# Retention's output with three pairs of each block as sevens and three low parts by transfer; one more seven in feed-forward 2, blocks 5 and 7

## The chip, the cores and the metric

The kernel runs on one core of a Trainium2 chip. The metric is the device time of one execution in microseconds (us). Engines are named as the profile names them: PE is the matrix engine, PEld its weight loads, DVE the vector engine, ACT the scalar engine, POOL GpSimd, and SP the engine that issues most of the transfers (DMA).

## The reference

One decoder layer in float32 for 256 tokens of 2048 features: a first half feed-forward, two token mixers side by side, a second half feed-forward, and a gated per-layer embedding, each followed by a layer normalisation. What the change touches:

```python
ret_branch = (jax.nn.silu(rg) * ro) @ w_ret_out[i]
...
mixed = (jax.nn.sigmoid(gate_r) * ret_branch + jax.nn.sigmoid(gate_a) * att_branch) @ w_mix_out[i]
h = layer_norm(alpha * h + mixed, ln_g[i, 1], ln_b[i, 1])
h = layer_norm(alpha * h + 0.5 * swiglu(h, w_ffn2_gu[i], w_ffn2_down[i]), ln_g[i, 2], ln_b[i, 2])
```

`w_ret_out` and `w_mix_out` are 2048 x 2048; `w_ffn2_gu` is 2048 x 11264.

## The kernel before, in words

**Two halves of a number.** Every float32 product is made of three matmuls. A value is split into a high part, which PE takes as it is, and a low part, the value less its high part. `Sum.add` (L407 to L420) issues, for a product of two such pairs, low times high, high times high and high times low into one bank (L418, L419, L420). All matmuls in question have a moving operand of 128x512.

**Chunks and units.** Weights come in chunks of 128x1024 float32 (512 KB), loaded by SP (L113). The weights of a matrix product of 2048 rows are walked in eight pairs p = 0 to 7 of 256 rows, and each pair has two chunks (n = 0, 1) for a block of 1024 columns. A unit is what is taken in one go:

- `Single` (P, L153): one chunk. ACT casts the high part (L124), DVE subtracts for the low part (L128). 12 matmuls; a pair is two such units, 24 matmuls.
- `Transferred` (T, L170): the second chunk of a pair. ACT writes the negative of the raw chunk, rounded as PE takes it (L133), and POOL issues a transfer that adds the raw chunk to it in place (L134): what is left is the low part, made without DVE. ACT casts the high part afterwards. It begins three units ahead of its use (`lead = 3`). The first chunk of a T pair is a `Single`.
- `Seven` (S, L181): both chunks of a pair as one, with seven block products in place of eight (Strassen's scheme, in the form that shares sums). 21 matmuls. DVE makes four sums of 128x512 (L208, L209, L210, L213), four low parts (L128, L215, L216, L217); ACT makes four casts (L124, L199, L211, L214). It needs forms of the other operand, made once for two pairs by `forms_of` (L504 adds, L492 to L495, and a split at L99 and L100).
- `Prepared` (D, L228): a seven whose sums were made and written to DRAM long before. It loads 2.75 MB (a chunk, half of the other, and four sums, L113, L236, L240) and costs DVE two low parts (L128, L252).

A `block` (L448) takes a list of units in order, a letter and a pair each, and accumulates their products into banks; at the end of its last seven `seven_common` (L523: one ACT copy L526, four DVE operations L527 to L530) folds the shared sums, and then DVE adds what the plain units left in the banks. `units_of` (L511) gives the letters S the pairs of a given list, the letters D those that were prepared ahead, and P and T the rest in order.

**Order.** The engines run the program in its order, each its own part. All loads stand in a plan that runs over the whole kernel, so that SP issues loads of the next blocks as slots come free; a load waits for its slot's last reader. After every unit taken, `run_side` (L354) takes one job off a list, `side`, that holds small work beside the matmuls; `along(n, job)` (L942) puts a job n units ahead. So side jobs go by units finished, across the bounds of blocks.

**The mixers' end.** `mixers` (L1193) ends with: the gate blocks; the attention output in four steps (banks ma0 to ma3, operands att_t), after whose second the retention forms `made[0]` are made (tiles mrf); the retention output in two blocks mr0 and mr1, `mixer_block` (L1207), each over eight pairs of `w_ret2`, in the order RET_UNITS; and the mix product, `w_mix`, in four blocks (banks mo0 to mo3). `mixer_block` ends with four additions on DVE (L1214: the shared result tiles eve, evw plus the banks mr1a, mr1b); then each half is multiplied with its gate sig (L1575) and the attention's part is added (L1576). The results sig0 to sig3 are what the mix product takes; they have to be turned first, into mixt0 to mixt7. sig0 and sig1, ready after mr0, go by words through transposing transfers (`by_words`, `by_turns`, L1543 to L1551): a copy on ACT, a transfer by SP four units later, a join on ACT, and then the job `mixed` that splits the turned tile (high part L99 on ACT, low part L100 on DVE): mixt0 and mixt1 from sig0, mixt2 and mixt3 from sig1. Counted from mr1's first unit, that job runs after the 13th unit for sig0 and after the 14th for sig1. sig2 and sig3 are turned on PE (L1541, banks mxt) during the mix, as side jobs behind these. The first unit of mo0 takes mixt0, the second mixt1, the third mixt2, and so on.

**Feed-forward 2.** `ffn` (L971) walks eleven blocks j of 512 gate and 512 up columns; `gu_units` (L899) gives the order of units of each. Blocks 1 to 5 and 7 are in AHEAD and have prepared sevens, in pairs 4 and 5 (blocks 2 and 4 in pair 4 alone); SEVEN are the pairs 0 to 3 that can be sevens in place. Blocks 6 and 8 to 10 have the order PTSSPSST. The banks of block 5 are f2g5, f2u5 and f25s.

Of the kernel before, what the change touches and what calls it, by code (L numbers as in the profile page):

```python
# [41 lines left out]
SEVEN = (0, 1, 2, 3)  # L42

AHEAD = {1: (4, 5), 2: (4,), 3: (4, 5), 4: (4,), 5: (4, 5), 7: (4, 5)}
# [12 lines left out]
def layer(ctx: ExitStack, tc: tile.TileContext, io):  # L57
# [13 lines left out]
    def banks(name):  # L71
        return [bank(name + str(j)) for j in range(2)]

    def slot(shape, dt, name):
        return slots.tile(shape, dt, tag="slot", name=name)
# [364 lines left out]
    def block_units(units, keys):  # L440

        for kind, p in units:
            if kind in "PT":
                plan.extend((Transferred if kind == "T" and n else Single)(keys(n, p)) for n in range(2))
            else:
                plan.append((Seven if kind == "S" else Prepared)(keys(0, p), keys(1, p)))
# [38 lines left out]
    def seven_forms(full, hi, lo):  # L485


        a11, a21 = (full[:, 0::2, t * P : (t + 1) * P] for t in range(2))
        a12, a22 = (full[:, 1::2, t * P : (t + 1) * P] for t in range(2))
        raw = slot([P, 8, P], F32, "sums")  # L490
        f5, f6, f7, f3 = (raw[:, 2 * j : 2 * j + 2, :] for j in range(4))
        dve.tensor_tensor(f5, a21, a22, ALU.subtract)  # L492
        dve.tensor_tensor(f7, a11, a21, ALU.subtract)
        dve.tensor_tensor(f6, f5, a11, ALU.subtract)
        dve.tensor_tensor(f3, a12, f6, ALU.add)  # L495
        split(hi, lo, raw)
        return lambda e: [(hi[:, 2 * j + e, :], lo[:, 2 * j + e, :]) for j in range(4)]

    def whole(parts, name):

        full = slot([P, 4, S], F32, name)
        n = 4 // len(parts)
        for j, v in enumerate(parts):
            dve.tensor_tensor(full[:, n * j : n * j + n], v[:, :, :S], v[:, :, S:], ALU.add)  # L504
        return full

    def forms_of(parts, name):
        hi, lo = (slot([P, 8, P], F32R, name + w) for w in "hl")
        return seven_forms(whole(parts, name + "w"), hi, lo)

    def units_of(order, sevens, ahead=()):  # L511

        sevens, ahead = list(sevens), list(ahead)
        plain = [p for p in range(KD // 2) if p not in sevens + ahead]
        of = {"S": sevens, "D": ahead, "P": plain, "T": plain}
        return [(kind, of[kind].pop(0)) for kind in order]
# [25 lines left out]
    def paired_out(key, n_k, lhs, ps, before=None):  # L542

        sums = [Sum(ps[t], n_k) for t in range(2)]
        for c in range(n_k // 2):
            if before is not None and c % 2 == 0:
                before(c // 2)
            u = take(key + (c,))
            tokens_chunk(u.chunk, 2 * c, lhs, sums, (0, 1))
            done(u)  # L550
            run_side()
# [347 lines left out]
    def gu_units(name, j):  # L899
        if j == 0:  # L900
            return [("P", p) for p in range(KD // 2)]
        if name == "f2" and j in AHEAD:
            return units_of(*(("PPSDSDSP", SEVEN[:3]) if j % 2 else ("PPSSDSSP", SEVEN)), AHEAD[j])
        return units_of("PTSSPSST", SEVEN)

# [28 lines left out]
    def plan_ffn(name):  # L934
        for j in range(KF // 4):
            block_units(gu_units(name, j), gu_keys(name, j))
        first, second, held = down_units(HELD_PAIRS[name == "f2"])
        block_units(first, down_keys(name, 0))
        block_units(second, down_keys(name, 1))
        plan.extend(Single(down_keys(name, 1)(n, p)) for n in range(2) for p in held)  # L940
# [215 lines left out]
    SH_A = [i + 8 if i < 8 else i - 8 if i < 16 else i for i in range(32)]  # L1156

    GATE_UNITS = units_of("PPSSPSSP", (0, 1, 2, 3))
    RET_UNITS = units_of("PPPSPSPP", (0, 1))
    VALUE_UNITS = units_of("PSPSSPSP", (0, 1, 2, 3))  # L1160
    gate_keys = lambda b: lambda n, p: ("w_in_f2", 29 + 4 * b + 2 * n, p)
    value_keys = lambda n, p: ("w_rv", 1 + n, p)
# [2 lines left out]
    def plan_mixers():  # L1165
# [16 lines left out]
        for b in range(2):  # L1182
            block_units(RET_UNITS, ret_keys(b))
        for blk in range(4):
# [8 lines left out]
    def mixers(ht, norm, residual, keepers, away):  # L1193
# [10 lines left out]
        made = {}  # L1204
# [59 lines left out]
        ret_t = [None] * HR  # L1264
# [107 lines left out]
        for h in range(0, HR, 2):  # L1372
# [3 lines left out]
            g = slot([P, 2, 512], F32, f"rgs{h}")  # L1376
# [154 lines left out]
        def of_pairs(v, k):  # L1531
            a = v[k // 2][:, k % 2, :]
            return a[:, :S], a[:, S:]
# [26 lines left out]
        for j in range(4):  # L1560
            v = sig[4 + j]
            act.activation(v, v, AF.Sigmoid)
            pa = banks(f"ma{j}")
            paired_out(("w_att2", 2 * j), KD // 2, lambda k: of_pairs(att_t, k), pa)
            for t in range(2):
                dve.tensor_tensor(v[:, t], v[:, t], pa[t], ALU.mult)
            if j == 1:
                made[0] = forms_of(ret_t[:2], "mrf")
        for b in range(2):
            for v in sig[2 * b : 2 * b + 2]:  # L1570
                act.activation(v, v, AF.Sigmoid)
            pr = mixer_block(f"mr{b}", RET_UNITS, ret_keys(b), lambda k: of_pairs(ret_t, k))
            for n in range(2):
                j = 2 * b + n
# [345 lines left out]
```

## Time and profile before

| | us |
|---|---|
| median of three executions | 2248.71 (2248.48 to 2250.64) |
| the profiled execution, whole | 2247.44 |
| its span, first to last instruction | 2245.6 |
| mr0, on PE | 1275.60 to 1317.76 |
| mr1, on PE | 1317.76 to 1359.92 |
| feed-forward 2 block 5, on PE | 1664.6 to 1705.9 |
| feed-forward 2 block 7, on PE | 1747.8 to 1787.9 |
| mean granted clock of PE | 0.999 |

Times inside the kernel count from the span's start. Rows of the timeline show start, duration, engine, line, operation, tiles and, in brackets, how long the engine had been idle and what released it. Rows of the waits show the waiting engine and what it writes, whom it waited for, and the sum, the number and the longest. Matmuls overlap, so a row's duration is longer than the distance between two starts.

### The profile page before, as it was taken

The page shows a single profiled execution, that of the slowest core. Times are in us where ns is not written, and L with a number is a line of the kernel's source. Part 1 is how long each engine was busy: PE and PEld are TensorE (multiplying, and loading weights), DVE is VectorE, ACT ScalarE, POOL GpSimd, SP SyncE. Part 2 cuts the span into 40 slices and gives each one's busy share as a digit, 9 for nine tenths or more (in the row PEclk, how much of TensorE's full clock was granted, in tenths as well). Part 3 has the DMA queues.
Part 4 walks back from the last instruction along what each step waited for, and adds up shares of the span by engine and source line. Part 5 has one row for each costly group of instructions (what it writes and reads, how often), then busy time and mean ns, then how long its engine had stood idle before and what let it go on. Part 6 is the DMA issues. An engine that isn't in the chain of part 4 may idle for free.

```text
span 2245.6 us, 28810 instructions
## 1 busy us (share of the span) xinstructions
PE 2231.5 (99%) x10195; PEld 1846.5 (82%) x10195; DVE 1995.4 (89%) x2636; ACT 1390.7 (62%) x1642; POOL 26.7 (1%) x37
## 2 busy tenths in 40 slices
PE   9999999999999999999999999999999999999998
PEld 8888888888888788888788888788887887888887
DVE  7999999999988999898779778789998999889877
ACT  6776767766554644566866456456666677655543
POOL 0000000000000000000000000000000000000000
PEclk9999999999999999999999999999999999999999
DMA  9787887765677778986657579788979978656772
GB/s 316 225 262 241 230 257 234 225 243 182 224 286 262 242 258 306 308 254 206 191 164 246 170 218 322 260 289 258 319 241 273 311 228 248 220 195 219 289 266 73
DMA packets 285946, 548.22 MB, mean 244 GB/s; under 512 B 87644, under 2 KB 92124, under 8 KB 285800
## 3 DMA queue, kind: packets, MB, share of 16 engines
q1 hardware_dynamic: 279784, 529.11, 70.7%
q0 software_dynamic: 4032, 14.68, 3.5%
q10 hardware_dynamic: 1984, 2.58, 0.3%
q8 instruction: 80, 1.31, 0.2%
q14 instruction: 66, 0.54, 0.1%
HBM read 484.43 MB, written 29.36 MB: 229 GB/s over the span
## 4 chain that ended last, share of the span: by engine, by line
PE 90%; DVE 6%; DMA 2%; issue 1%; ACT 1%; ACTq 0%; DVEq 0%; SPq 0%; POOL 0%; POOLq 0%
PE f1g L420 3%; PE f1g L418 3%; PE f1g L419 3%; PE rqk L369 3%; PE f1u L420 2%; PE f1u L418 2%; PE f1u L419 2%; PE f2g L418 2%; PE f2g L420 2%; PE f2g L419 2%; PE f2u L418 2%; PE f2u L420 2%; PE f2u L419 2%; PE aqk L369 2%; PE f2d L420 2%; PE f1d L419 2%
## 5 line engine op out<-in xcount | busy, mean ns | idle before, releaser
L124 ACT CAST hf_gu<-rf_gu 128x1024 fp32r<-128x1024 f32 x264 | 271.4, 1047 | 45.5 <-DMA rf_gu<-in_f_gu 38.6
L128 DVE TENSOR_TENSOR lf_gu<-rf_gu,hf_gu 128x1024 fp32r<-128x1024 f32 x236 | 281.5, 1217 | 14.6 <-ACT hf_gu L124 13.4
L124 ACT CAST hf_down<-rf_down 128x1024 fp32r<-128x1024 f32 x150 | 153.0, 1050 | 61.1 <-DMA rf_down<-in_f_down 50.2
L128 DVE TENSOR_TENSOR lf_down<-rf_down,hf_down 128x1024 fp32r<-128x1024 f32 x150 | 178.0, 1218 | 13.1 <-ACT hf_down L124 5.9
L128 DVE TENSOR_TENSOR lw_in_f<-rw_in_f,hw_in_f 128x1024 fp32r<-128x1024 f32 x140 | 167.0, 1217 | 2.8 <-ACT hw_in_f L124 2.7
L124 ACT CAST hw_in_f<-rw_in_f 128x1024 fp32r<-128x1024 f32 x140 | 141.9, 1050 | 24.9 <-DMA rw_in_f<-in_w_in_f 14.9
L214 ACT CAST hvf_gu<-vf_gu 128x1024 fp32r<-128x1024 f32 x76 | 80.1, 1054 | 84.8 <-DVE vf_gu L213 75.1
L211 ACT CAST huf_gu<-uf_gu 128x1024 fp32r<-128x1024 f32 x76 | 80.0, 1053 | 53.8 <-DVE uf_gu L209 50.5
L216 DVE TENSOR_TENSOR luf_gu<-uf_gu,huf_gu 128x1024 fp32r<-128x1024 f32 x76 | 92.4, 1216 | 1.6 <-ACT huf_gu L211 1.6
L217 DVE TENSOR_TENSOR lvf_gu<-vf_gu,hvf_gu 128x1024 fp32r<-128x1024 f32 x76 | 92.4, 1216 | 0.0
L418 PE MATMUL f1g<-hf_gu,xt 128*128 128x512 f32 x232 | 90.7, 391 | 0.0
L419 PE MATMUL f1g<-hf_gu,xt 128*128 128x512 f32 x232 | 90.5, 390 | 0.0
L420 PE MATMUL f1g<-lf_gu,xt 128*128 128x512 f32 x232 | 90.5, 390 | 0.0
L418 PE MATMUL f2g<-hf_gu,ht 128*128 128x512 f32 x214 | 83.5, 390 | 0.0
L420 PE MATMUL f2g<-lf_gu,ht 128*128 128x512 f32 x214 | 83.3, 389 | 0.0
L419 PE MATMUL f2g<-hf_gu,ht 128*128 128x512 f32 x214 | 83.3, 389 | 0.0
L418 PE MATMUL f1u<-hf_gu,xt 128*128 128x512 f32 x192 | 74.7, 389 | 0.0
L419 PE MATMUL f1u<-hf_gu,xt 128*128 128x512 f32 x192 | 74.7, 389 | 0.0
L420 PE MATMUL f1u<-lf_gu,xt 128*128 128x512 f32 x192 | 74.7, 389 | 0.0
L418 PE MATMUL f2u<-hf_gu,ht 128*128 128x512 f32 x168 | 65.7, 391 | 0.0
L420 PE MATMUL f2u<-lf_gu,ht 128*128 128x512 f32 x168 | 65.4, 389 | 0.0
L419 PE MATMUL f2u<-hf_gu,ht 128*128 128x512 f32 x168 | 65.4, 389 | 0.0
(1622 smaller groups left out, 6729.0 us busy)
## 6 DMA issues: line engine op xcount, KB each, us to landing
rf_gu<-in_f_gu SPq DMA_DIRECT2D x360, 512.0 KB
rf_down<-in_f_down SPq DMA_DIRECT2D x176, 512.0 KB
rw_in_f<-in_w_in_f SPq DMA_DIRECT2D x148, 512.0 KB
rw_rv<-in_w_rv SPq DMA_DIRECT2D x32, 512.0 KB
rw_ret<-in_w_ret SPq DMA_DIRECT2D x32, 512.0 KB
rw_mix<-in_w_mix SPq DMA_DIRECT2D x32, 512.0 KB
rw_pg<-in_w_pg SPq DMA_DIRECT2D x32, 512.0 KB
lf_gu<-rf_gu POOLq DMA_DIRECT2D x28, 512.0 KB, 7.8
```

The lines of the kernel that those rows point to most:

```text
L124: act.copy(self.hi, self.raw)
L128: dve.tensor_tensor(self.lo, self.raw, self.hi, ALU.subtract)
L211: act.copy(uh, u)
L214: act.copy(vh, v)
L216: dve.tensor_tensor(ul, u, uh, ALU.subtract)
L217: dve.tensor_tensor(vl, v, vh, ALU.subtract)
L369: pe.matmul(ps[f], hi[:, kk, f * P : (f + 1) * P], rhs(k), start=k == 0, stop=k == n_k - 1,)
L418: pe.matmul(o, al, bh, start=first, stop=False)
L419: pe.matmul(o, ah, bh, start=False, stop=False)
L420: pe.matmul(o, ah, bl, start=False, stop=self.left == 0)
```

## The change

The order of units of the retention output goes from PPPSPSPP with pairs 0 and 1 as sevens to PTSTSTSP with pairs 0, 1 and 2 as sevens: per block one plain pair becomes a seven, and of the five pairs that stay plain three have the low part of their second chunk made by transfer. The third seven's pair needs a second set of forms, `made[1]`, from ret_t[2:4]; it is made after the last step of the attention output. Feed-forward 2 blocks 5 and 7 go from PPSDSDSP with three sevens in place to PSDSSDSP with four. Blocks 1 and 3 keep their order: of the blocks in AHEAD, `j > 4` selects 5 and 7.

```diff
         if name == "f2" and j in AHEAD:
+            if j > 4:
+                return units_of("PSDSSDSP", SEVEN, AHEAD[j])
             return units_of(*(("PPSDSDSP", SEVEN[:3]) if j % 2 else ("PPSSDSSP", SEVEN)), AHEAD[j])
...
-    RET_UNITS = units_of("PPPSPSPP", (0, 1))
+    RET_UNITS = units_of("PTSTSTSP", (0, 1, 2))
...
-            if j == 1:
-                made[0] = forms_of(ret_t[:2], "mrf")
+            if j in (1, 3):
+                g = j // 2
+                made[g] = forms_of(ret_t[2 * g : 2 * g + 2], f"mrf{g}")
```

A retention block has 13 units in place of 14, a changed feed-forward block 10 in place of 11. On PE the program has 9,970 rows in place of 9,982.

On DVE, at the end of mr1, the rows before. lw_mix_0_3 and lw_mix_0_4 are low parts of the mix's weights, eve and evw the result tiles of mr1, sig2 and sig3 the gates:

```order
L128 TENSOR_TENSOR lw_mix_0_3_12265<-rw_mix_0_3_12178,hw_mix_0_3_12237 128x1024
L100 TENSOR_TENSOR mixt2_12269<-mxraw1_12128,mixt2_12269 128x2x256
L100 TENSOR_TENSOR mixt3_12272<-mxraw1_12128,mixt3_12272 128x2x256
L1214 TENSOR_TENSOR eve_12180<-eve_12180,mr1a0_11924 128x512
L1214 TENSOR_TENSOR eve_12180<-eve_12180,mr1b0_11926 128x512
L1214 TENSOR_TENSOR evw_12181<-evw_12181,mr1a1_11925 128x512
L1214 TENSOR_TENSOR evw_12181<-evw_12181,mr1b1_11927 128x512
L1575 TENSOR_TENSOR sig2_10380<-sig2_10380,eve_12180 128x1024
L1576 TENSOR_TENSOR sig2_10380<-sig2_10380,eve_11222 128x1024
L1575 TENSOR_TENSOR sig3_10574<-sig3_10574,evw_12181 128x1024
L1576 TENSOR_TENSOR sig3_10574<-sig3_10574,evw_11223 128x1024
L128 TENSOR_TENSOR lw_mix_0_4_12302<-rw_mix_0_4_12203,hw_mix_0_4_12263 128x1024
```

The same place on DVE in the changed program (its lines have numbers 2 or 3 higher there):

```order
L1216 TENSOR_TENSOR eve_12254<-eve_12254,mr1a0_11952 128x512
L1216 TENSOR_TENSOR eve_12254<-eve_12254,mr1b0_11954 128x512
L1216 TENSOR_TENSOR evw_12255<-evw_12255,mr1a1_11953 128x512
L1216 TENSOR_TENSOR evw_12255<-evw_12255,mr1b1_11955 128x512
L1578 TENSOR_TENSOR sig2_10380<-sig2_10380,eve_12254 128x1024
L1579 TENSOR_TENSOR sig2_10380<-sig2_10380,eve_11222 128x1024
L1578 TENSOR_TENSOR sig3_10574<-sig3_10574,evw_12255 128x1024
L1579 TENSOR_TENSOR sig3_10574<-sig3_10574,evw_11223 128x1024
L128 TENSOR_TENSOR lw_mix_0_4_12334<-rw_mix_0_4_12250,hw_mix_0_4_12293 128x1024
L100 TENSOR_TENSOR mixt2_12338<-mxraw1_12184,mixt2_12338 128x2x256
L100 TENSOR_TENSOR mixt3_12341<-mxraw1_12184,mixt3_12341 128x2x256
```

The split into mixt2 and mixt3 has moved from in front of mr1's last additions to behind them, the gate operations and a low part of the mix's weights.

On SP, in feed-forward 2 block 5, the rows before, of pair 1 (a seven), pair 5 (prepared), pair 2 (the last seven) and pair 7 (plain):

```order
L113 DMA rf2_gu_5_0_1_14965<-in_f2_gu 128x2x512
L113 DMA rf2_gu_5_1_1_14967<-in_f2_gu 128x2x512
L113 DMA rf2_gu_5_0_5_15057<-in_f2_gu 128x2x512
L236 DMA rf2_gu_5_0_5b_15059<-in_f2_gu 128x2x256
L240 DMA huf2_gu_5_0_5_15061<-hudf2_gu_5_0_5_8927 128x1024
L240 DMA luf2_gu_5_0_5_15063<-ludf2_gu_5_0_5_8928 128x1024
L240 DMA hvf2_gu_5_0_5_15065<-hvdf2_gu_5_0_5_8929 128x1024
L240 DMA lvf2_gu_5_0_5_15067<-lvdf2_gu_5_0_5_8930 128x1024
L113 DMA rf2_gu_5_0_2_15097<-in_f2_gu 128x2x512
L113 DMA rf2_gu_5_1_2_15099<-in_f2_gu 128x2x512
L113 DMA rf2_gu_5_0_7_15122<-in_f2_gu 128x2x512
```

The same place on SP in the changed program, where pair 2 and pair 3 are sevens and pair 3 is the last:

```order
L113 DMA rf2_gu_5_0_1_14954<-in_f2_gu 128x2x512
L113 DMA rf2_gu_5_1_1_14956<-in_f2_gu 128x2x512
L113 DMA rf2_gu_5_0_2_14970<-in_f2_gu 128x2x512
L113 DMA rf2_gu_5_1_2_14972<-in_f2_gu 128x2x512
L113 DMA rf2_gu_5_0_5_15102<-in_f2_gu 128x2x512
L236 DMA rf2_gu_5_0_5b_15104<-in_f2_gu 128x2x256
L240 DMA huf2_gu_5_0_5_15106<-hudf2_gu_5_0_5_8927 128x1024
L240 DMA luf2_gu_5_0_5_15108<-ludf2_gu_5_0_5_8928 128x1024
L240 DMA hvf2_gu_5_0_5_15110<-hvdf2_gu_5_0_5_8929 128x1024
L240 DMA lvf2_gu_5_0_5_15112<-lvdf2_gu_5_0_5_8930 128x1024
L113 DMA rf2_gu_5_0_3_15145<-in_f2_gu 128x2x512
L113 DMA rf2_gu_5_1_3_15147<-in_f2_gu 128x2x512
```

Two chunks of pair 2 have come in front of the six loads of the prepared pair 5, and the last seven behind these is pair 3.

## Prediction

> **What bounds the kernel now.** The profile's page was read first: TensorE (PE) is at work nearly all the time.
>
> ```profile
> span 2245.6 us, 28810 instructions
> PE 2231.5 (99%) x10195; PEld 1846.5 (82%) x10195; DVE 1995.4 (89%) x2636; ACT 1390.7 (62%) x1642; POOL 26.7 (1%) x37
> ```
>
> The profiled execution took 2247.44 us, 1.8 more than its span and 1.3 less than the median of 2248.71. Sums below are made against the execution and carried over to the median. Second, PE's timeline gives the price of a matmul, here at the seam between the two retention-output blocks mr0 and mr1:
>
> ```profile
> 1317.53 0.39 PE L420 MATMUL mr0b<-lw_ret,rett 128*128 128x512 f32 x1
> 1317.76 0.39 PE L418 MATMUL mr1a<-hw_ret,rett 128*128 128x512 f32 x1
> ```
>
> Each row shows 0.39 us, but starts are 0.227 apart; that is what one costs. A plain weight unit (12 matmuls) is 2.72 us, a seven (21) 4.76 us where its plain pair (24) is 5.44. Third, the waits of PE: the longest and two of the ends of sevens that speak below; those left out are of 1.4 us and less each, so hardly any idle time can be won back.
>
> ```profile
> PE lnps L670 <- DVE mixy L658: 2.0, 2, 1.5
> ...
> PE f25s L420 <- DVE luf_gu L216: 0.4, 1, 0.4
> PE f26s L420 <- DVE luf_gu L216: 0.3, 1, 0.3
> ```
>
> So what counts is the number of matmuls, and whether DVE, which makes the low parts, stays ahead. Fourth, the windows of the two stages that are touched (mr0, mr1; then feed-forward 2 blocks 5, 6, 7; columns PE, PEld, DVE, ACT, POOL busy, then PE's granted clock, full in all, DMA's share, GB/s):
>
> ```profile
> 1275.60:1317.80 42.20, 42.20 (x188) 34.95 (x187) 31.99 (x37) 21.97 (x23) 0.00 (x0) 1.00 0.62 200
> 1317.80:1359.90 42.10, 42.10 (x187) 34.87 (x186) 37.53 (x43) 27.81 (x31) 0.00 (x0) 1.00 0.79 252
> ...
> 1664.60:1705.90 41.30, 40.71 (x178) 33.08 (x177) 33.70 (x42) 25.86 (x29) 0.86 (x1) 1.00 0.88 289
> 1705.90:1747.80 41.90, 41.41 (x182) 33.65 (x181) 40.02 (x49) 29.53 (x32) 0.86 (x1) 1.00 0.87 258
> 1747.80:1787.90 40.10, 40.10 (x178) 33.21 (x177) 34.80 (x43) 25.54 (x29) 0.89 (x1) 1.00 0.89 296
> ```
>
> DVE has some 10 us to spare in mr0, 4.6 in mr1, 7.6 in block 5, 5.3 in block 7, and 1.9 in block 6.
>
> **The matmuls removed.** Four new sevens, each for a plain pair, remove 3 matmuls each: 12 x 0.227 = 2.72 us, 1.36 in retention, 0.68 in each of blocks 5 and 7. That is 0.12%, less than the 0.2% (4.5 us) which a measurement of this kernel can tell from no change.
>
> **Retention's units.** A seven's DVE work, and what it costs more than a plain pair, stands in block 5's last seven: from the first row's start to the last row's is 6.42 us; the two low parts of a pair are 2.27 (2.35 less the overlap).
>
> ```profile
> 1690.82 0.69 DVE L208 TENSOR_TENSOR uf_gu<-rf_gu 128x512 f32<-128x512 f32 x1 [6.29 <-DMA rf_gu<-in_f_gu]
> ...
> 1697.24 2.35 DVE L128 TENSOR_TENSOR lf_gu<-rf_gu,hf_gu 128x1024 fp32r<-128x1024 f32 x2
> ```
>
> Per block, DVE had 12 low parts (13.6 us) and 2 sevens (12.9): 26.5. It now has 7 low parts (7.9), since three are transferred, and 3 sevens (19.3): 27.2. The surplus of 0.7 disappears in the spare time above. A second set of forms is added at the end of the attention output, which the rows of the first set price:
>
> ```profile
> 1254.64 1.29 DVE L504 TENSOR_TENSOR mrfw<-rett 128x512 f32<-128x512 f32 x2
> ...
> 1259.84 2.35 DVE L128 TENSOR_TENSOR lw_att<-rw_att,hw_att 128x1024 fp32r<-128x1024 f32 x2
> ```
>
> That is 5.2 us of DVE from the first row to the last, a wait on ACT in it, from about 1276.4 on, in front of mr0's first seven. This seven now begins on PE at 1275.6 + 4 x 2.72 = 1286.5 and needs its first sum's low part about 2 us later; DVE can have it at 1276.4 + 5.2 + 5.3 = 1286.9. It holds by about 1.6 us: nothing on the path. If that cover is gone, it costs what it is late.
>
> The six transferred low parts leave DVE and are a multiplication on ACT and an accumulating transfer, whose rows in feed-forward are:
>
> ```profile
> L133 ACT ACTIVATE lf_gu<-rf_gu x2: 1054/1056/1057, 1699.3 to 1732.2; 128x1024 fp32r<-128x1024 f32 x2
> ...
> lf_gu<-rf_gu POOLq DMA_DIRECT2D x28, 512.0 KB, 7.8
> ```
>
> They start three units ahead. In retention those are, for the last two, a plain unit, a seven and a plain unit: 2.72 + 4.76 + 2.72 = 10.2 us, for 1.05 + 7.8 = 8.85. With 1.3 us in hand, and ACT's queue in front, a late one costs 0 to 2 us. DMA has room there (shares 0.62 and 0.79 above). I take 0.3 for all six, near nothing, since none of that row's 28 stands among PE's waits.
>
> **The hidden cost: one unit less in mr1.** The side jobs go by units finished. mr1 now has 13 instead of 14 units, and the job that splits the second gated tile into mixt2 and mixt3 runs on the 14th, after the first unit of the mix. Thus on DVE it now stands behind the four additions that end mr1 (L1214), the four gate operations (L1575, L1576) and one low part. The prices are at the end of mr0, where PE went on with mr1 at 1317.76:
>
> ```profile
> 1317.96 0.69 DVE L1214 TENSOR_TENSOR evw<-evw,mr0b 128x512 f32<-128x512 f32 x1
> ...
> 1323.36 2.35 DVE L128 TENSOR_TENSOR lw_ret<-rw_ret,hw_ret 128x1024 fp32r<-128x1024 f32 x2
> ...
> 1358.35 1.29 DVE L100 TENSOR_TENSOR mixt<-mxraw,mixt 128x512 fp32r<-128x512 f32 x2 [2.00 <-ACT mixt L99]
> ```
>
> With E the end of mr1 on PE: the gate operations end at E + 5.60 (1323.36 - 1317.76), the low part takes 1.14 (half of the pair's 2.27), mixt2's low part 0.68: E + 7.42. PE has two units of the mix without mixt2, 2 x 2.72 = 5.44 us, and must then wait: 1.98 us. In before the split ran at 1358.35, in front of L1214 and 7 us ahead of its use. The order on DVE is fixed, and its last addition cannot come before PE's last matmul of mr1, so I see no way round this; after it mixt3 (0.6 more) is in time.
>
> A stop of PE may also cost clock. These rows are PE's at its wait in the value product, and at the normalisation behind the mix:
>
> ```profile
> 774.63 0.40 PE L419 MATMUL rvss<-huw_rv,rvf1h 128*128 128x512 f32 x1
> 776.35 0.50 PE L420 MATMUL rvss<-luw_rv,rvf1h 128*128 128x512 f32 x1 [1.32 <-DVE luw_rv L216]
> ...
> 778.29 0.62 PE L420 MATMUL rvss<-luw_rv,rvf1h 128*128 128x512 f32 x1
> 778.71 0.63 PE L418 MATMUL rvsa<-hw_rv,ht 128*128 128x512 f32 x1
> ...
> 781.70 0.40 PE L419 MATMUL rvsb<-hvw_rv,ht 128*128 128x512 f32 x1
> ...
> 1448.67 0.39 PE L420 MATMUL mo<-lw_mix,mixt 128*128 128x512 f32 x1
> 1450.60 0.44 PE L670 MATMUL lnps<-ident,mixy 128*128 128x128 f32 x2 [1.55 <-DVE mixy L658]
> ...
> 1452.03 0.39 PE L419 MATMUL pp<-hw_pp,pt 128*128 128x512 f32 x1
> ```
>
> After the first, of 1.72 us between starts, matmuls stood 0.43 apart for 3.4 us: 8 matmuls at 0.2 more, 1.6 to 1.7 us lost. After the second, of 1.93, there was nothing. So the range is 0 to 1.7; by one case in two I leave it out of the likeliest sum and make it a rival. [...]
>
> **Blocks 5 and 7.** DVE's work rises by 6.42 - 2.27 = 4.15 us in each. Its waits there are the cover:
>
> ```profile
> DVE uf_gu L208 <- DMA rf_gu<-in_f_gu: 6.3, 1, 6.3
> DVE lf_gu L128 <- ACT hf_gu L124: 1.2, 1, 1.2
> ...
> DVE uf_gu L208 <- DMA rf_gu<-in_f_gu: 4.0, 1, 4.0
> DVE lf_gu L128 <- ACT hf_gu L124: 1.1, 1, 1.1
> ```
>
> (the first two of block 5, the last two of block 7.) 7.5 and 5.1 us cover 4.15, if the last seven's chunks land when they did. They stand on SP behind the six loads of the second prepared seven:
>
> ```profile
> 1675.68 0.37 SPq L113 DMA_DIRECT2D rf_gu<-in_f_gu  x1
> ...
> 1679.76 2.03 SPq L113 DMA_DIRECT2D rf_gu<-in_f_gu  x2
> ```
>
> They landed 11 us later (1690.82, above), and from then DVE was behind: PE's waits in f25s and f26s follow. The new order moves the prepared loads behind two more chunks of the new seven; they wait for a slot that PE frees when the first seven ends (1674.4 by my count instead of 1675.7), and the last chunks for the end of the first prepared one (1679.6 instead of 1679.8). So the landing moves by -1.5 to 0 us in block 5; in block 7, whose gap is smaller, by -0.3 to +1.9. As the DVE chain behind each landing sets PE's time, the 0.68 us of matmuls saved ahead of it is not kept: PE waits in f25s instead. Together I take 0, between -1.8 and +1.9.
>
> **The sum** on the profiled execution: -1.36 (retention's matmuls) + 1.98 (mixt2) + 0.3 (transfers) + 0 (blocks 5, 7) = +0.9: 2248.3; on the median 2249.6.
>
> **The rivals.**
> - *All matmuls kept, no new wait*: mixt2 is in time by something I overlook, and blocks 5 and 7 keep their savings: -2.72, 2246.0. For it: PE-bound page; against it: DVE's order. Chance 0.10. If the waits of f25s and f26s go as well (about 2.2 us with what follows them), 2243.8: 0.03.
> - *The wait costs clock too*: +0.9 + 1.7 = 2251.3. For it the value product, against it the normalisation. Chance 0.25.
> - *Blocks 5 and 7 land late* (the other side): if the last seven's chunks land over 3.6 us later in total, DVE's chain, with 1.9 us spare in block 6 and no more behind block 7, hands all of it to PE, and the kernel is slower than 2253.2; with 2.6 later in each, +0.9 + 5.2: 2254.8. Against it: SP issues them no later by my count. Chance 0.07.
> - *Transfers late*: ACT's queue puts each of the six back by 2.3 us, 1 more than is in hand: six times 1 us instead of the 0.3, so 2249.6 + 5.7 = 2255.3. Against it: the 28 of before, of which none holds PE. Chance 0.04.
>
> **The numbers.** Forecast 0.51, +0.9: 2249.6. From the first rival to a little above the clock rival, with the unknown of blocks 5 and 7: 2246.0 to 2252.9 leaves out some 0.17. Faster by over 0.2% (below 2244.2) 0.03; slower (above 2253.2) 0.10; within 0.87.
>
> **What would show it.** PE: 9,970 matmul rows of code for 9,982; a wait of about 2 us at the mix's third unit (mo, L418) put down to DVE mixt L100; mr0 and mr1 0.68 us shorter each, without a wait on rf or lw_ret transfers; half-spaced matmuls behind the wait or none. DVE: idle before L208 down to some 2 us in block 5 and about 1 in block 7. It is wrong if no such wait stands there, or if the waits at the last sevens, f25s to f210s, sum to over 2 us more or less than before.

## The result, and the profile after

The changed kernel takes 2252.41 us (median of 20 executions, 2251.15 to 2255.21), the kernel before on the same chip 2248.33 (20 executions). The ratio is 1.0017, with a 95% interval of 1.0010 to 1.0023: slower by 3.8 us (2.2 to 5.2). That is within the range, within 0.2%, and on the side that was forecast, but four times the 0.9 of the sum. Microseconds beside a ratio are, from here on, the ratio's distance from 1 times 2248.5.

The profiled execution of the changed kernel took 2252.14 us (before: 2247.44). The page's head, to be held against the first rows of the prediction:

```profile
span 2250.4 us, 28851 instructions
PE 2232.2 (99%) x10183; PEld 1843.8 (82%) x10183; DVE 2008.4 (89%) x2661; ACT 1402.5 (62%) x1657; POOL 31.9 (1%) x43
```

Twelve matmuls fewer, as planned, and yet PE is busy for 0.7 us longer: either matmuls have become slower or the rows of idle time have not caught all. Where the time went is read from the starts of stages on PE, each the first matmul of its bank in PE's timeline:

| stage begins on PE | before | after | later by |
|---|---|---|---|
| mr0 | 1275.60 | 1275.29 | -0.31 |
| mr1 | 1317.76 | 1316.77 | -0.99 |
| mr1 ends (0.227 after the start of its last matmul) | 1359.92 | 1358.25 | -1.67 |
| normalisation after the mix (lnps) | 1450.60 | 1456.78 | +6.18 |
| feed-forward 2 block 5 | 1664.61 | 1670.81 | +6.20 |
| block 6 | 1705.90 | 1710.44 | +4.54 |
| block 7 | 1747.79 | 1751.58 | +3.79 |
| block 8 | 1787.91 | 1791.66 | +3.75 |
| end of the span | 2245.6 | 2250.4 | +4.8 |

Retention gains what its matmuls promised (0.68 in each of mr0 and mr1). The mix alone loses 7.85 us. Blocks 5 to 7 give 2.45 back. The mix first: the longest waits of PE in the changed kernel.

```profile
PE mo L418 <- DVE mixt L100: 4.2, 2, 2.2
PE lnps L670 <- DVE mixy L658: 1.9, 2, 1.4
```

The first row is new, and there are two such waits where one was forecast. Neither f25s nor f26s stands among the waits any more. PE's timeline from the end of mr1 to the mix's third unit, and the mix's end:

```profile
1358.03 0.39 PE L420 MATMUL mr1b<-lw_ret,rett 128*128 128x512 f32 x1
1360.45 0.79 PE L418 MATMUL mo<-hw_mix,mixt 128*128 128x512 f32 x1 [2.04 <-DVE mixt L100]
...
1363.18 0.63 PE L418 MATMUL mo<-hw_mix,mixt 128*128 128x512 f32 x1
1363.61 0.52 PE L419 MATMUL mo<-hw_mix,mixt 128*128 128x512 f32 x1
...
1367.38 0.39 PE L420 MATMUL mo<-lw_mix,mixt 128*128 128x512 f32 x1
1369.97 0.50 PE L418 MATMUL mo<-hw_mix,mixt 128*128 128x512 f32 x1 [2.21 <-DVE mixt L100]
...
1370.82 0.63 PE L418 MATMUL mo<-hw_mix,mixt 128*128 128x512 f32 x1
1371.25 0.63 PE L419 MATMUL mo<-hw_mix,mixt 128*128 128x512 f32 x1
...
1454.99 0.39 PE L420 MATMUL mo<-lw_mix,mixt 128*128 128x512 f32 x1
```

The starts give the price, less the 0.23 that a matmul takes anyway. The first stop, at the mix's first unit, is 1360.45 - 1358.03 - 0.23 = 2.19; the second, at the third unit, 1369.97 - 1367.38 - 0.23 = 2.36. Behind each, matmuls last 0.63 and stand 0.43 apart instead of 0.23 (1363.18 to 1363.61; 1370.82 to 1371.25), and the two stretches lose 1.70 and 1.72 us. Together 7.97, against 7.85 up to the normalisation (6.18 + 1.67, by the table) and 7.99 up to the mix's last matmul, which comes 6.32 later than the 1448.67 of before. So the mix's loss is accounted for: two stops and the clock behind both. It also explains PE's busy time: the half-speed matmuls count in it with their longer rows (in the window 1360.48 to 1363.88, at a granted clock of 0.50, PE is busy for all 3.40 us with 8 matmuls).

Why the second stop is there is what the prediction said. DVE's timeline of the changed kernel:

```profile
1359.71 1.29 DVE L100 TENSOR_TENSOR mixt<-mxraw,mixt 128x512 fp32r<-128x512 f32 x2 [0.31 <-ACT mixt L99]
1360.92 0.68 DVE L1216 TENSOR_TENSOR eve<-eve,mr1a 128x512 f32<-128x512 f32 x1
...
1366.96 1.23 DVE L1579 TENSOR_TENSOR sig<-sig,evw 128x1024 f32<-128x1024 f32 x1
1368.10 1.22 DVE L128 TENSOR_TENSOR lw_mix<-rw_mix,hw_mix 128x1024 fp32r<-128x1024 f32 x1
1369.24 1.28 DVE L100 TENSOR_TENSOR mixt<-mxraw,mixt 128x512 fp32r<-128x512 f32 x2
```

The second L100 is the split into mixt2 and mixt3, behind the additions, the gate operations and one low part, and PE resumes 0.73 after it begins. The first L100 is the split into mixt0 and mixt1, which the prediction did not walk through: it runs 1.46 us after PE's end of mr1 (1358.25), where in before it ran 6.0 ahead of that end (1359.92):

```profile
1353.92 1.29 DVE L100 TENSOR_TENSOR mixt<-mxraw,mixt 128x512 fp32r<-128x512 f32 x2 [0.46 <-ACT mixt L99]
```

It is late because of ACT. Two rows of ACT in before, and two in the changed kernel:

```profile
1347.72 1.05 ACT L124 CAST hw_mix<-rw_mix 128x1024 fp32r<-128x1024 f32 x1 [1.97 <-DMA rw_mix<-in_w_mix]
...
1353.27 1.14 ACT L99 CAST mixt<-mxraw 128x512 fp32r<-128x512 f32 x2
```

```profile
1352.76 1.05 ACT L124 CAST hw_mix<-rw_mix 128x1024 fp32r<-128x1024 f32 x1 [2.74 <-PE mr1b L419]
...
1359.05 1.15 ACT L99 CAST mixt<-mxraw 128x512 fp32r<-128x512 f32 x2
```

ACT is held up at a cast of the mix's weights, 5.0 us later than before, and the rest of its queue (the copies of the turned words, L99) comes 5.8 later. The row names PE as the releaser of that cast, but the cast also waited for its own load, which the trace's semaphore records have landing at 1352.66; the wait was over at 1352.72, and the matmul named ended at 1352.75. So the load held it. SP's timeline has the loads, first of before, then of the changed kernel (SPq rows last as long as SP stands at the issue: the first transposing one of before ends at 1339.17, the next issue begins at 1339.22):

```profile
1334.52 4.65 SPq L961 DMA_TRANSPOSE mx0t<-mx0w  x1
1339.22 0.57 SPq L113 DMA_DIRECT2D rw_mix<-in_w_mix  x1
1339.89 3.57 SPq L961 DMA_TRANSPOSE mx1t<-mx1w  x1
1343.51 6.05 SPq L113 DMA_DIRECT2D rw_mix<-in_w_mix  x7
```

```profile
1332.64 6.52 SPq L963 DMA_TRANSPOSE mx0t<-mx0w  x1
1339.26 0.53 SPq L113 DMA_DIRECT2D rw_ret<-in_w_ret  x1
1339.89 2.17 SPq L113 DMA_DIRECT2D rw_mix<-in_w_mix  x2
1342.17 6.55 SPq L963 DMA_TRANSPOSE mx1t<-mx1w  x1
1348.81 3.04 SPq L113 DMA_DIRECT2D rw_mix<-in_w_mix  x6
```

The transposing transfers hold SP for 13.07 us where they held it for 8.22, and the mix's loads behind the second are issued 5.3 us later. That delay runs through: load, cast on ACT, L99, L100 on DVE, PE. A second way leads to the same split. ACT's copy L526, which opens the fold of mr1's last seven, also stands behind that cast and runs at 1353.71, though the sum that it copies was complete at 1348.9; DVE stands idle for it, and then folds and makes two low parts ahead of L100:

```profile
1354.32 0.69 DVE L527 TENSOR_TENSOR evw<-eve,mr1s 128x512 f32<-128x512 f32 x1 [3.05 <-ACT eve L526]
```

Blocks 5, 6 and 7 of feed-forward 2 in the changed kernel, as windows (columns as in the prediction), and the waits of DVE in block 5 that are left:

```profile
1670.80:1710.40 39.60, 39.60 (x175) 32.58 (x174) 37.63 (x47) 27.33 (x30) 0.86 (x1) 1.00 0.96 306
1710.40:1751.60 41.20, 41.16 (x182) 33.73 (x182) 39.30 (x50) 29.03 (x32) 0.86 (x1) 1.00 0.84 267
1751.60:1791.70 40.10, 39.97 (x176) 32.40 (x175) 39.59 (x49) 27.62 (x31) 0.86 (x1) 1.00 0.94 293
```

```profile
DVE lf_gu L128 <- ACT hf_gu L124: 1.7, 1, 1.7
```

DVE works 3.9 us more in block 5 (37.63 for 33.70) and 4.8 more in block 7 (39.59 for 34.80), and its idle time in front of L208, 6.3 and 4.0 before, is gone altogether: the last seven's first row no longer waits for its load.

```profile
1695.32 0.69 DVE L208 TENSOR_TENSOR uf_gu<-rf_gu 128x512 f32<-128x512 f32 x1
```

It starts 24.5 us after block 5's start on PE; in before it started 26.2 after it (1690.82 - 1664.61).

### The profile page after: what moved, and what is told of

Same layout as the page of the kernel before. It is cut to its first block, busy times and chain, and to the rows that moved or that the text cites. A ratio compares the mean times of both kernels' runs of the same rounds, so it can differ in the third digit from the quotient of the medians.

```text
span 2250.4 us, 28851 instructions
## 1 busy us (share of the span) xinstructions
PE 2232.2 (99%) x10183; PEld 1843.8 (82%) x10183; DVE 2008.4 (89%) x2661; ACT 1402.5 (62%) x1657; POOL 31.9 (1%) x43
## 4 chain that ended last, share of the span: by engine, by line
PE 90%; DVE 5%; DMA 2%; issue 1%; ACT 1%; SPq 0%; ACTq 0%; DVEq 0%
PE rqk L369 3%; PE f1g L420 2%; PE f1g L418 2%; PE f1g L419 2%; PE f2g L418 2%; PE f2g L419 2%; PE f2g L420 2%; PE f1u L418 2%; PE f1u L419 2%; PE f1u L420 2%; PE f2u L418 2%; PE f2u L419 2%; PE f2u L420 2%; PE aqk L369 2%; PE f2d L420 2%; PE f2d L418 2%
## 5 line engine op out<-in xcount | busy, mean ns | idle before, releaser
L418 PE MATMUL f2g<-hf_gu,ht 128*128 128x512 f32 x208 | 81.2, 390 | 0.0
L419 PE MATMUL f2g<-hf_gu,ht 128*128 128x512 f32 x208 | 80.9, 389 | 0.0
L369 PE MATMUL rqk<-ht,hw_in_f 128*128 128x512 f32 x256 | 64.3, 392 | 0.0
L418 PE MATMUL f2u<-hf_gu,ht 128*128 128x512 f32 x160 | 62.6, 391 | 0.0
```

The costliest lines, as they stand in the source:

```text
L369: pe.matmul(ps[f], hi[:, kk, f * P : (f + 1) * P], rhs(k), start=k == 0, stop=k == n_k - 1,)
L418: pe.matmul(o, al, bh, start=first, stop=False)
L419: pe.matmul(o, ah, bh, start=False, stop=False)
```

## The experiments

Ratios compare each kernel with the kernel before on the same chip; after them stands the 95% interval.

### Which part costs

**ret_only**: the retention part of the change alone.

```diff
-            if j > 4:
-                return units_of("PSDSSDSP", SEVEN, AHEAD[j])
```

> The retention part of the change alone; feed-forward 2 keeps its order of before. Theory (side jobs one unit later): the two waits at the mix's first and third unit and the half-speed spells behind both stay as in the changed kernel, and retention's 6 matmuls are saved: about +6.2 us on before, as far as the changed kernel's trace is behind at the end of the mix. Rival (the change as a whole, feed-forward 2 among it, costs the 4 us): about +2 us.

Measured: 2254.56 us (11 executions), 1.0035 (1.0025 to 1.0046), +7.9 us. PE's waits:

```profile
PE mo L418 <- DVE mixt L100: 5.4, 2, 3.8
```

The whole loss is retention's. The two stops at the mix are there without the feed-forward part, of 1.76 and 3.95 us by the starts, with half speed behind the second alone. The trace is of the fastest execution, 2252.17, 4.8 behind before's by the span; four of the eleven took 2259.8 to 2263.6, and what these lost is in no trace.

**f2_only**: the feed-forward part alone.

```diff
-    RET_UNITS = units_of("PTSTSTSP", (0, 1, 2))
+    RET_UNITS = units_of("PPPSPSPP", (0, 1))
...
-            if j in (1, 3):
-                g = j // 2
-                made[g] = forms_of(ret_t[2 * g : 2 * g + 2], f"mrf{g}")
+            if j == 1:
+                made[0] = forms_of(ret_t[:2], "mrf")
```

> Blocks 5 and 7 alone, with retention as before. By the changed kernel's trace, where PE's distance to before shrinks by 2.4 us over blocks 5 to 7: about -2.4 us, and no wait of PE in f25s and f26s over 0.2. By the forecast (what the matmuls save is taken back by DVE's chain behind a late landing): 0, between -1.8 and +1.9, with the waits in f25s and f26s about as before.

Measured: 2245.96 us (11), 0.9994 (0.9985 to 1.0003), -1.3 us. No stop at the mix. In its profile blocks 5 to 7 gain some 2.1 us, and DVE waits for no load of theirs; f26s keeps a wait of 0.6. So blocks 5 and 7 don't cost; a gain of their 1.36 lies within the interval, and so does nothing at all. (The profiled execution, 2247.28, had a mean granted clock of 0.998, before's 0.999.) The profile of ret_only raises a doubt on the 2.45 of the changed kernel: there, with blocks 5 and 7 as before, blocks 5 to 7 gained 2.25 too, DVE's wait for loads being 7.5 us in sum instead of 10.3. It is the only such trace. From the start of block 5 to that of block 8 the traces of the nine kernels with the new order of units are 2.1 to 2.6 us shorter than before's, among them mr0_transfer_earlier below (2.56), in which feed-forward 2 begins within 0.1 us of before. With the old order, before_later, before_transfer and order_earlier_ret below differ by -0.09, +0.15 and -0.21, though PE is 3.7 to 14 us late there. So the gain goes with the order of units and not with PE being late; why ret_only has it is not known.

### The second stop

**before_later**: the kernel before, with only the job of sig0 and sig1 one unit later.

```diff
-                    along(2 + n, lambda n=n: by_words(n))
+                    along(3 + n, lambda n=n: by_words(n))
```

> The kernel before with the chain of side jobs for sig0 and sig1 begun one unit later, so that mixt2's split stands behind mr1's additions as in the changed kernel, with retention's units as they were. Theory (place of the side jobs): a wait of about 2.0 us at the third unit, put down to mixt, and 0 to 1.7 of clock: +2.0 to +3.7 us; whether the first unit waits too tells if the place alone makes that one or the later loads of mr1's end are needed. Rival (the load of mr1): no wait, 0 us.

Measured: 2251.42 us (11), 1.0015 (1.0006 to 1.0024), +3.4 us. Its wait, and PE's rows at it:

```profile
PE mo L418 <- DVE mixt L100: 1.9, 1, 1.9
```

```profile
1365.30 0.39 PE L420 MATMUL mo<-lw_mix,mixt 128*128 128x512 f32 x1
1367.56 0.50 PE L418 MATMUL mo<-hw_mix,mixt 128*128 128x512 f32 x1 [1.87 <-DVE mixt L100]
...
1368.37 0.63 PE L418 MATMUL mo<-hw_mix,mixt 128*128 128x512 f32 x1
```

One stop, 2.03 us by the starts, at the third unit, then eight matmuls at half speed (1.7 us). Together 3.7 for the 3.4 (1.3 to 5.4) measured. With the retention blocks untouched, the place of the job makes the second stop, at the price that was forecast (1.98) and the clock beside it. There is no first stop: being a unit later alone does not make mixt0 late.

**after_earlier**: the changed kernel with the job back at its old distance from mr1's end.

```diff
-                    along(2 + n, lambda n=n: by_words(n))
+                    along(1 + n, lambda n=n: by_words(n))
```

> The changed kernel with the chain of side jobs for sig0 and sig1 begun one unit earlier. Theory (the place of the side jobs alone makes both waits): neither wait at the mix, no half-speed spell, 7.9 us back: about -3.8 us on before. Rival (three sevens and the transfers in mr1 bring the mix's chunks and its casts too late in any order): at least the first wait stays, with its clock, about +0 us.

Measured: 2250.25 us (11), 1.0007 (0.9998 to 1.0016), +1.6 us.

```profile
PE mo L418 <- DVE mixt L100: 1.8, 1, 1.8
```

The second stop is gone and the first stays (1.96 by the starts, seven matmuls at half speed behind it). So the place of the job makes the second and not the first. L99 is in time here, 1.8 us ahead of the end of mr1. But the join's copies on ACT now stand in front of the fold's copy L526, which runs only at 1355.18, and DVE's fold waits for it, with the split behind the fold: the job moved forward moves into the same queue on ACT.

### The first stop

**no_transfer**: the changed kernel with three sevens, but without transferred low parts in the retention output; the side jobs stay late.

```diff
-    RET_UNITS = units_of("PTSTSTSP", (0, 1, 2))
+    RET_UNITS = units_of("PPSPSPSP", (0, 1, 2))
```

> The changed kernel with retention's order PPSPSPSP: three sevens, none of the six low parts by transfer. If the transfers had a part in the waits at the mix (ACT's multiplications, GpSimd's traffic): the first wait shrinks, over 1 us better than the changed kernel. If the place of the last seven and of the side jobs makes them: both waits stay, within 1 us of the changed kernel or slower, by what DVE's three more low parts per block add.

Measured: 2249.22 us (10), 1.0004 (0.9996 to 1.0013), +0.9 us. The wait, then SP's two transposing transfers, then the first split and addition of DVE:

```profile
PE mo L418 <- DVE mixt L100: 3.6, 1, 3.6
```

```profile
1331.57 5.67 SPq L963 DMA_TRANSPOSE mx0t<-mx0w  x1
...
1338.95 6.22 SPq L963 DMA_TRANSPOSE mx1t<-mx1w  x1
```

```profile
1356.09 1.29 DVE L100 TENSOR_TENSOR mixt<-mxraw,mixt 128x512 fp32r<-128x512 f32 x2 [0.35 <-ACT mixt L99]
1357.30 0.68 DVE L1216 TENSOR_TENSOR eve<-eve,mr1a 128x512 f32<-128x512 f32 x1
```

The first stop is gone without the transfers and their multiplications on ACT. mixt0's split runs 1.1 us ahead of PE's end of mr1 (1357.17); its distance to that end was -6.0 in before, -4.0 with the job alone one unit later (before_later), -1.1 here, +1.5 in the changed kernel. So the transfers bring the last 2.6 us, and only these make a stop of it; the job's place and the third seven had used up the 6. On SP, the six mix loads behind the second transposing transfer are issued 11.9 us ahead of the end of mr1 here and 9.4 in the changed kernel. Of these 2.5 us, 1.2 lie in the transposing transfers (11.89 here, 13.07 there) and 1.3 in the two mix loads between them (0.88 here, 2.17 there). The 11.89 are already 3.7 more than before's 8.22, with no accumulating transfer near; the job's later place alone has 8.48 (before_later), the third seven alone 8.46 (no_transfer_earlier, below), and why both together have more was not tried. The second stop is longer here (3.74 by the starts, instead of 2.0): the late first split stands in front of DVE's additions, which begin at 1357.30, whereas at the end of mr0 in before all but the last had run by PE's end. By the rows, -1.36 in retention, -2.5 in blocks 5 to 7, 3.74 for the stop and 1.7 for the half speed behind it make +1.6, against a measured +0.9 (-0.9 to +2.9).

**before_transfer**: the kernel before, with transfers in mr1 as the only change (two sevens, the same number of units and matmuls).

```diff
-    RET_UNITS = units_of("PPPSPSPP", (0, 1))
+    RET_UNITS = [units_of(u, (0, 1)) for u in ("PPPSPSPP", "PTPSTSTP")]
...
-            block_units(RET_UNITS, ret_keys(b))
+            block_units(RET_UNITS[b], ret_keys(b))
...
-            pr = mixer_block(f"mr{b}", RET_UNITS, ret_keys(b), lambda k: of_pairs(ret_t, k))
+            pr = mixer_block(f"mr{b}", RET_UNITS[b], ret_keys(b), lambda k: of_pairs(ret_t, k))
```

> The kernel before, two sevens per block and side jobs as they were, with three low parts of mr1 by transfer (order PTPSTSTP). Theory (transfers and transposing transfers hold each other up): the two transposes, 4.65 and 3.57 us of SP in before, take over 5 us each, mixt0's split comes 2 us and more later before its use than in before; time +0 to +3 us, by whether that reaches PE. Rival (the transposes are longer only for the loads of the third seven): they take what they took in before, 0 us.

Measured: 2253.3 us (10), 1.0022 (1.0013 to 1.0031), +4.9 us.

```profile
PE mxt L1541 <- DVE sig L1576: 3.3, 1, 3.3
```

```profile
1334.86 5.15 SPq L961 DMA_TRANSPOSE mx0t<-mx0w  x1
...
1340.73 5.81 SPq L961 DMA_TRANSPOSE mx1t<-mx1w  x1
...
1346.64 3.72 SPq L113 DMA_DIRECT2D rw_mix<-in_w_mix  x7
```

Three transfers in one block cost 4.9 us (2.9 to 7.0) by themselves, more than the 0 to 3 expected, in a kernel where they take 3.4 us of work off DVE. The two transposing transfers hold SP for 10.96 us instead of 8.22, the mix's loads come 3.1 later, and ACT and DVE with them. Both splits still come in time for their units, but now they delay the additions and the gates, and PE waits for sig2 and sig3 when it wants to turn them (mxt), 3.49 by the starts, and half speed behind it, to 1372.9, costs 2.6 more.

**order_only**: in mr1 the transfers moved later, PSTSTSTP, so that the first seven begins sooner.

```diff
-    RET_UNITS = units_of("PTSTSTSP", (0, 1, 2))
+    RET_UNITS = [units_of(u, (0, 1, 2)) for u in ("PTSTSTSP", "PSTSTSTP")]
```

(and RET_UNITS[b] at its two uses, as above, here and below.)

> The changed kernel with mr1's units in the order PSTSTSTP, so that four units follow its last seven, as in before, and not two; the side jobs stay one unit late. Theory now (the first wait comes from the end of mr1: the last plain chunk and the mix's chunks are issued behind two transposing transfers that hold SP for 4 to 6.5 us each, and ACT's copy for the last seven stands behind their casts; the second wait from the side jobs' place): the first wait goes, the second stays with 2.0 us and its clock, so about 4 us better than the changed kernel, 0 on before. Rival (the side jobs' place makes the first wait too): both stay, +4 us.

Measured: 2258.52 us (6), 1.0049 (1.0035 to 1.0063), +11.0 us. The first wait of PE, and SP's two transposing transfers:

```profile
PE mr1a L420 <- DMA lw_ret<-rw_ret: 7.6, 2, 6.5
```

```profile
1336.65 10.33 SPq L963 DMA_TRANSPOSE mx0t<-mx0w  x1
...
1347.76 14.22 SPq L963 DMA_TRANSPOSE mx1t<-mx1w  x1
```

What I expected of the order was wrong. With the accumulating transfers later in the block, both kinds are late: PE waits 7.6 us for two of the transferred low parts, 6.5 for one of them, where in the changed kernel it waits for none (they land 4.7 to 8.9 us after their issue there), and the transposing transfers hold SP for 24.6 us instead of 13.07. The mix's tiles are late as well. The trace is of the slowest of the six executions, 2263.56.

**order_earlier**: the same order, with the job one unit earlier (`along(1 + n, ...)`).

> Both remedies: mr1 in the order PSTSTSTP and the side jobs begun one unit earlier, in the changed kernel. Theory (two causes, one for each wait): no wait at the mix, no half-speed spell; 7.9 us better than the changed kernel, about -3.8 us on before. Rival (something else at the end of mr1, DVE's own backlog, makes the first wait): at least 2 us of it stay.

Measured: 2254.53 us (11), 1.0032 (1.0019 to 1.0045), +7.2 us. No wait for mixt is left, but PE stands for 4.0 us in mr1 itself, at a transferred low part. The transposing transfers hold SP for 8.13 and 5.21.

**order_earlier_ret**: the same without the feed-forward part.

> Both remedies, and feed-forward 2 as before: tells what blocks 5 and 7 give once retention is mended. If they give their matmuls and the waits of f25s and f26s: 2 us slower than with them. If those waits go by the shift of retention alone, as the trace of the retention part alone has it: under 1 us slower than with them, the matmuls' 1.36 at the most.

Measured: 2261.31 us (12; 2253.69 to 2272.43), 1.0061 (1.0044 to 1.0079), +13.7 us. It tells little on blocks 5 and 7: its profiled execution was already 4.5 us late in front of mr0, and the executions spread by 19 us. It says only that this order stays bad.

### Both stops away

**no_transfer_earlier**: three sevens, no transfers, job one unit earlier.

```diff
-    RET_UNITS = units_of("PTSTSTSP", (0, 1, 2))
+    RET_UNITS = units_of("PPSPSPSP", (0, 1, 2))
...
-                    along(2 + n, lambda n=n: by_words(n))
+                    along(1 + n, lambda n=n: by_words(n))
```

> The changed kernel without transferred low parts in retention (order PPSPSPSP) and with the side jobs begun one unit earlier. Theory now (the first wait needs the transfers, the second the side jobs' place): no wait at the mix and no half-speed spell; 5 us better than without the transfers alone, about -4 us on before, 2244.5. Rival (the last seven so near the end leaves too little time in any case): a first wait of 1 to 2 us with its clock stays, -1 us.

Measured: 2247.47 us (11), 0.9995 (0.9986 to 1.0004), -1.1 us.

```profile
PE mxt L1543 <- DVE sig L1579: 2.0, 1, 2.0
```

Neither split is late. In their place PE now waits for sig2 and sig3, 2.11 by the starts, and no matmul behind that is at half speed. Ahead of the fold DVE stands idle for 2.99 us, for ACT's copy L526, which runs at 1352.92 behind three casts of the mix's weights and the join's copies; the sum that it copies was complete at 1348.5.

**mr0_transfer_earlier**: as the one above, but with transfers in mr0, where no transposing transfer runs.

```diff
-    RET_UNITS = units_of("PTSTSTSP", (0, 1, 2))
+    RET_UNITS = [units_of(u, (0, 1, 2)) for u in ("PTSTSTSP", "PPSPSPSP")]
...
-                    along(2 + n, lambda n=n: by_words(n))
+                    along(1 + n, lambda n=n: by_words(n))
```

> As the run without transfers and with the side jobs earlier, but with the three transfers of mr0 put back. Theory (only mr1's transfers meet the transposing transfers, which run in mr1): within 1 us of that run, about -4 us on before. Rival (the transfers cost by themselves, wherever they are): 2 us slower than it.

Measured: 2247.29 us (11), 0.9997 (0.9988 to 1.0006), -0.7 us. Transfers in mr0 cost nothing that can be measured (-0.7 with them, -1.1 without); in mr1, where the transposing ones run, three cost 4.9 (before_transfer). The wait at mxt is 2.0 again.

**turns_later**: the same, with the turning of sig2 and sig3 on PE a unit later.

```diff
-            side.append(idle)
+            side.extend([idle, idle])
```

> As the run with mr0's transfers alone and the side jobs earlier, with one idle side job more in front of the turns of sig2 and sig3, so that PE asks for sig2 a unit later. Theory (what is left at the mix is that PE reaches the first turn, mxt, 2.0 us before DVE has finished sig2): that wait goes and nothing takes its place, 2 us better than that run, about -4.4 us on before, some 2243.5. Rival (the later turns make mixt4 late for the fifth unit): a wait there instead, 0 to 2 us, no gain.

Measured: 2248.57 us (11), 1.0002 (0.9993 to 1.0011), +0.4 us. PE's rows at its wait, and behind it:

```profile
1373.12 0.50 PE L418 MATMUL mo<-hw_mix,mixt 128*128 128x512 f32 x1 [2.00 <-DVE mixt L100]
1373.46 0.39 PE L419 MATMUL mo<-hw_mix,mixt 128*128 128x512 f32 x1
1373.69 0.39 PE L420 MATMUL mo<-lw_mix,mixt 128*128 128x512 f32 x1
```

The wait has moved two units on, to mixt4, with the same length, and DVE works without a break from 1354.40 until it has made that tile. So it is not the place of the turning that holds PE, but DVE's chain around the end of mr1 (fold, splits, additions, gates, then the tiles from sig2): with the third seven it ends some 2 us too late, at either place where PE asks for it. In all three kernels of this part DVE is idle for 3.0 us in front of that chain, for L526; whether the stop goes when L526 runs as soon as its sum is complete was not tried. No version here is measurably faster than the kernel before; the two with the job earlier and no transfers in mr1 are faster than the changed kernel (0.9995 and 0.9997 against 1.0017, intervals apart).

## Why the prediction came out as it did

**Right: the matmuls of retention.** -0.68 in each block, by the starts of mr0, mr1 and the mix; the second set of forms made no wait in mr0.

**Right: the second stop.** The mechanism was the side job that goes by units, and before_later shows it by that alone. The size was 1.98; the runs have 2.03 (before_later) and 2.36 (the changed kernel, in which PE asks for mixt2 3.9 us later, by the first stop and its clock, and DVE's gates end 4.3 later than forecast, at 1368.10 instead of 1358.25 + 5.60).

**Mis-sized: the clock behind the stop.** The likeliest sum had 0, with a rival of 1.7 at 0.25. It was 1.70 and 1.72, behind both stops, and 1.7 in before_later. From two rows that contradicted each other the sum took the cheap one, and by the prediction's own "one case in two" it could as well have held the other.

The granted clock (the share of full speed that PE was given) tells more. In the changed kernel it falls to 0.50 for 3.41 us, from 1360.47 and from 1370.71, each time 1.71 us of full speed; in before it falls to 0.50 for 3.41 us from 778.28, behind the first of the prediction's two rows (and in both once more at the very end, from 2247.94 and 2242.60). In these two traces all its changes lie whole multiples of 3.41 us apart (1, 2 and 1 between the four in the changed kernel's mix). Cut the two traces into steps of 3.41 us at these changes: PE was idle for 2.04 and 2.21 us in the steps ahead of the changed kernel's two half-speed ones, for 1.49 in the step ahead of before's, and for 1.55 in the step of before's stop at the normalisation, behind which there is none. The other kernels' stops in the mix, by PE's rows, have half speed behind them after 1.87 us idle (before_later) and 1.80 (after_earlier), and none after 1.60 (ret_only's first), 1.95 (no_transfer_earlier) and 2.00 (turns_later). So of two stops of some 2 us one cost clock and the other not, and the length alone does not tell which. The steps lie differently in the two executions (the clock's first record begins 6.87 us after the span's start in before, 5.38 in the changed kernel); that it goes by where a stop falls among them is my estimate, and was not shown.

**Failed: "I take 0.3 for all six" transfers, and the first split not walked through.** The step looked for a wait on the transferred low parts themselves (lw_ret), and in the changed kernel there is none. The cost came through another queue, SP's: with the transfers the mix's loads are issued 2.5 us later against the end of mr1 than in no_transfer (1.2 in the transposing transfers, 1.3 in the loads between them), and behind these loads stand ACT's cast, L526 and L99, DVE's fold and the split into mixt0. This is the first stop with its clock, 2.19 + 1.70 = 3.9 us. Runs show that it needs the transfers (no_transfer), that transfers in mr1 alone cost 4.9 (before_transfer) and that in mr0 nothing can be measured of them (mr0_transfer_earlier). The path through SP and ACT is read from the traces. The prediction walked the job one unit later only for mixt2; the one ahead of it had moved by the same unit, and its 6 us in hand went to three things at once. Why the transposing transfers hold SP longer in a block with accumulating ones (5.15 and 5.81 in before_transfer, 4.65 and 3.57 in before) was not shown.

**Too careful: blocks 5 and 7.** Given 0 (-1.8 to +1.9); in the trace blocks 5 to 7 gained 2.45. The step that failed is that the last seven's chunks land no sooner and DVE's chain behind the landing sets PE's time. The landing stopped mattering: L208 starts 1.7 us earlier within the block and without a wait, and f25s and f26s no longer wait. f2_only confirms by its time that nothing is lost (-1.3, -3.4 to +0.7), not the size; the size is 2.1 to 2.6 in nine traces.

**The account.** -1.67 to the end of mr1, 0.31 of which lay ahead of mr0; +7.85 in the mix; -2.45 in blocks 5 to 7; +1.1 in small differences behind block 8, which were not followed: +4.8 by span, 4.7 by the profiled executions, 3.8 (2.2 to 5.2) by the ratio. The rivals of slower blocks 5 and 7 did not happen. That of late transfers did in kind, at another place than it named and for 3.9 us instead of 5.7; and of the first rival one part came, the waits of f25s and f26s that go. Of the signs of being wrong none came: the wait at the third unit stands there, and the waits from f25s to f210s changed by some 1 us. (DVE's idle time at L208, forecast to fall to some 2 and 1 us, went to nothing.) That the time lies inside the range is in part luck. The 3.9 of a stop that had no term and the 1.7 of clock that the sum left out are 5.6 us too many; the 2.45 that blocks 5 to 7 gave, against a 0, hide near half of it.

## What to carry to other kernels

When a change alters how many units a block has, list every job that is counted in units across its end, and walk each through all its queues (SP, ACT, DVE), not only the one that looks latest. The three transfers of before_transfer, for none of which PE waited, cost 4.9 us: of a transfer that relieves a busy engine ask which other transfers share its time, and what is queued behind those. Where DVE's chain behind a block's last matmul feeds the next stage, a stop can be moved from tile to tile without growing shorter (2.0 us at mxt in mr0_transfer_earlier, 2.0 at mixt4 in turns_later); look at what that chain itself waited for when it began, here one small copy far back in ACT's queue.

## What the runs showed of the hardware

Transposing transfers took longer in a block with accumulating ones. One held SP for 3.57 to 4.79 us in before and before_later; for 5.15 and 5.81 in before_transfer, where three accumulating transfers in the same block are the only change; and for 10.33 and 14.22 in order_only, where these stand later in the block, and where PE waited 7.6 us for two of them. But with three sevens, and no accumulating transfer in mr1, it took 1.76 and 6.70 as well (no_transfer_earlier; 5.67 and 6.22 in no_transfer), so the accumulating ones are not the whole of it; what else counts was not shown.

PE's clock fell to half for 3.41 us at a time in before and in the changed kernel (at the end of the span apart), and only at bounds of steps of 3.41 us. One stretch of half-speed rows lost some 1.7 us behind stops of 1.96 (after_earlier), 2.03 (before_later), 2.19 and 2.36 (the changed kernel) and 3.74 us (no_transfer); a longer one lost 2.6 (before_transfer, a stop of 3.49) and some 3 (ret_only, a stop of 3.95), and there the first row behind the stop was already slow (0.80 us in ret_only, 0.50 in before_later). Behind 1.95 and 2.00 us idle (no_transfer_earlier, turns_later) there was no half speed. So a stop of 2 us cost 2 us or 3.7. If a stop costs clock when 1.8 us of it lie in one step (1.80 idle in after_earlier did; the 1.49 of before says that less can do), then by an estimate from these figures a stop of 2 us costs clock in 0.53 of the places where it can fall, (3.41 - 1.8 + 0.2) / 3.41; one profile alone doesn't price it.
